# RMS norms of a two-layer encoder: the sum of squares of eight chunks taken from TensorE (eight ones-products) to GpSimd (seven f32 adds) and one ones-product

## The chip, the cores and the metric

The kernel runs on all eight cores of one Trainium2 chip, one batch element on each core, with no exchange between cores. The metric is device time in microseconds (us) of the slowest core, and a smaller number is better. Some runs fell into a second, slower state (about 1565 to 1795 us here, whatever the kernel): the cores of one die, or of both, show a lower granted clock in it. A "fast" run is one outside this state.

## The reference, cut to what matters

Five norms of this form stand in the network, over `x` of 2048 tokens by 1024 features per core:

```python
def rms_norm(x, g):
    xf = x.astype(jnp.float32)
    y = xf * lax.rsqrt(jnp.mean(xf * xf, axis=-1, keepdims=True) + EPS)
    return (y * g.astype(jnp.float32)).astype(x.dtype)

# layer 0:  x += attention(rms_norm(x))   norm 0    x += mlp(rms_norm(x))   norm 1
# layer 1:  x += conv(rms_norm(x))        norm 2    x += mlp(rms_norm(x))   norm 3
# output:   rms_norm(x)                   norm 4
def sq_relu_mlp(h, w_up, w_down):
    a = jax.nn.relu(h @ w_up)
    return (a * a) @ w_down
```

## The kernel before

Features lie on partitions: `x` is eight chunks of 128 partitions, in f32, and tokens are cut into four tiles of 512. A norm of one tile follows the tile's last matrix product. For each of eight chunks a matmul result is added to `x` on VectorE (`add_x`), the chunk is squared, and a product with a matrix of ones sums the squares over partitions. The eight ones-products accumulate in PSUM bank 7. Then ScalarE makes 1/rms of it (Ln, Exp), and eight `scalar_tensor_tensor` (STT below) on VectorE write `x * gain * rstd`.

```python
def norm_tile(gidx, src, c0, n, bank, out_fn, pool=False):
    for c in range(8):
        xa, xr = src(c)
        o, r_ = h_ap(c, c0, n), h_r(c, c0, n)
        alts = [("act", ... AF.Square ...), ("dve", ... i * i ...)]     # cut
        p.op(alts, None, [xr], [r_], None)
        MMS([(PS(bank, 0, n), onesN, o, c == 0, c == 7)], [CR1, r_], [PR(bank)])
    nb_ = nrs[ni[0] % 2]
    ni[0] += 1
    rs = nb_.ap[:, 0:n]
    ACT(rs, PS(bank, 0, n), AF.Ln, [PR(bank), sm.r()], [nb_.r(0, n)], n, bias=eps_ap)
    ACT(rs, rs, AF.Exp, [nb_.r(0, n)], [nb_.r(0, n)], n, scale=-0.5, ps=False)
    for c in range(8):
        out_fn(gidx, c, c0, n, src(c), nb_)

def norm_to_hT(gidx, c, c0, n, src, nb_):
    STT(h_ap(c, c0, n), src[0], gain_of(gidx, c),                       # shortened
        nb_.ap[:, 0:n], ALU.mult, ALU.mult, [...], [h_r(c, c0, n)], n)

def add_x(tt, c, lo, n, b):
    xa, xr = xs(tt, c, lo, n)
    TT("dve", xa, xa, PS(b, 0, n), ALU.add, [xr, PR(b)], [xr], n)

# the end of attention (norm 1); the ends of MLP 0 (norm 2), the convolution (norm 3)
# and MLP 1 (norm 4) have the same form
for tt in range(4):
    ...
    for oc in range(8):
        b = main.next()
        wo_mm(b, oc, tt, range(6), 0)
        wo_mm(b, oc, tt, (6, 7), 1)
        add_x(tt, oc, 0, 512, b)
    norm_x(1, tt, 0, 512, norm_to_hT)

# the start of an MLP
ACT(r.ap, PS(b), AF.Relu, [PR(b)], [r.r()], 512)
TT("pool", aT[i].ap[:, lo:lo + 512], r.ap, r.ap, ALU.mult, ...)
```

A list scheduler places the operations in the program, with an estimated cost for each, and so fixes one order of instructions per engine. An operation with alternatives gets its engine there too. At run time each engine follows its order and waits on semaphores. Matmul results go round seven PSUM banks.

## Time and profile before

| | before |
|---|---|
| time, median of 3 | 1534.3 us (1533.86 to 1534.9) |
| TensorE busy | 1471.2 us, 7312 matmuls |
| VectorE busy | 576.6 us |
| ScalarE busy | 490.7 us |
| GpSimd busy | 380.3 us |
| one 128x512 matmul | 0.2159 us |
| one STT of 128x512 | 0.74 us |

The first fence has three lines of the page of the kernel before: busy time, share and count of instructions of each engine; the chain of work that ended last, by engine; and the group of all STTs (L336 is the line of the STT helper): busy us, mean ns of one, then idle time of VectorE in front of them.

```profile
PE 1471.2 (96%) x7312; PEld 684.8 (45%) x7312; DVE 576.6 (38%) x820; ACT 490.7 (32%) x777; POOL 380.3 (25%) x387
...
PE 93%; DMA 2%; DVE 1%; ACT 1%; issue 1%; SPq 0%; POOL 0%; DVEq 0%; ACTq 0%; POOLq 0%
...
L336 DVE SCALAR_TENSOR_TENSOR arena<-arena 128x512 bf16<-128x512 f32 (+2 forms) x232 | 157.8, 738 | 24.8 <-ACT arena L328 19.7
```

TensorE is the bound, and GpSimd is idle for three quarters of the span. The chain in order of time (start, length, what) holds one piece that runs from the MLP of layer 0 through norm 2 and the convolution to the end of norm 3. L317 is the matmul helper:

```profile
412.63 663.21 PE psum L317 x3072
```

That is 663.21 / 3072 = 0.2159 us per matmul with nothing between them. A ones-product taken out of this piece shortens it by 0.2159 us, if nothing else changes.

The timeline of VectorE gives the four bursts of eight STTs that close the four tiles of norm 2:

```profile
798.55 5.38 DVE L336 SCALAR_TENSOR_TENSOR arena<-arena 128x512 bf16<-128x512 f32 x8
813.26 5.39 DVE L336 SCALAR_TENSOR_TENSOR arena<-arena 128x512 bf16<-128x512 f32 x8 [0.45 <-ACT arena L328]
829.63 5.38 DVE L336 SCALAR_TENSOR_TENSOR arena<-arena 128x512 bf16<-128x512 f32 x8
843.91 5.39 DVE L336 SCALAR_TENSOR_TENSOR arena<-arena 128x512 bf16<-128x512 f32 x8 [3.84 <-ACT arena L328]
```

Each takes 5.4 us. A tile gives VectorE eight adds of at most 0.69 us, this burst and at most one square: 11.6 us or less, in a tile of 72 matmuls, 15.5 us. VectorE has room.

The lines are of the convolution, from the timelines of both engines: a GpSimd product alone, then an STT and a GpSimd product that starts under it.

```profile
859.87 1.16 POOL L333 TENSOR_TENSOR arena<-arena 128x512 bf16<-128x512 bf16 x1 [4.02 <-DVE arena L336]
...
883.88 0.74 DVE L336 SCALAR_TENSOR_TENSOR arena<-arena 128x512 f32<-128x512 f32 x1
...
884.12 1.52 POOL L333 TENSOR_TENSOR arena<-arena 128x512 bf16<-128x512 bf16 x1 [0.18 <-DVE arena L336]
```

The GpSimd product takes 0.36 us longer; the STT still had 0.50 us to run when it began.

### The profile page before, as it was taken

How to read it: one execution, taken by the hardware profiler on the slowest of the kernel's cores; microseconds unless marked ns; L12 is line 12 of the kernel's file. 1: busy time of each engine (PE TensorE's matmuls, PEld its weight loads, DVE VectorE, ACT ScalarE, POOL GpSimd, SP SyncE). 2: the span in 40 equal slices, each digit the busy share in tenths (PEclk: the TensorE clock that was granted, in tenths of full speed). 3: DMA queues.
4: the chain of work that ended last, by engine and by line, in shares of the span. 5: the costliest groups of instructions: out<-in, count | busy, mean ns of one | idle time of the engine just before them, and what ended most of it. 6: DMA issues, size and time to landing. Idle time of an engine off the chain costs nothing.

```text
span 1531.6 us, 19902 instructions; the slowest of 8 cores (1524.7 to 1531.6 us)
## 1 busy us (share of the span) xinstructions
PE 1471.2 (96%) x7312; PEld 684.8 (45%) x7312; DVE 576.6 (38%) x820; ACT 490.7 (32%) x777; POOL 380.3 (25%) x387
## 2 busy tenths in 40 slices
PE   5999997699999999999999999999999999999997
PEld 2656443243344444444444444444444444444445
DVE  4646677556114013013036444456123023032047
ACT  3566686343320220310334333333310310301333
POOL 5100000100350540630620223210530621612600
PEclk8999999589999999999999999999999999999999
DMA  9944445630330420410410433310410411312014
GB/s 252 186 86 100 86 114 110 186 76 1 55 56 1 70 42 0 83 28 2 75 22 1 62 42 49 56 28 7 76 28 3 81 28 24 60 28 49 8 55 166
DMA packets 60910, 95.00 MB, mean 62 GB/s; under 512 B 3792, under 2 KB 40912, under 8 KB 58768
## 3 DMA queue, kind: packets, MB, share of 16 engines
q0 software_dynamic: 52016, 69.18, 25.9%
q1 hardware_dynamic: 8800, 24.55, 5.2%
q8 instruction: 61, 1.00, 0.3%
q14 instruction: 33, 0.27, 0.1%
HBM read 127.37 MB, written 8.52 MB: 89 GB/s over the span
## 4 chain that ended last, share of the span: by engine, by line
PE 93%; DMA 2%; DVE 1%; ACT 1%; issue 1%; SPq 0%; POOL 0%; DVEq 0%; ACTq 0%; POOLq 0%
PE psum L317 93%; DMA arena<-scr 2%; ACT arena L328 1%; DMA arena<-xT 1%; DVE arena L336 1%; DVE arena L333 1%; ACT arena L343 0%; SPq L349 0%; DMA scr<-arena 0%; POOL arena L349 0%; DVE arena L424 0%; DVE arena L345 0%; ACT arena L423 0%; DVEq L216 0%; ACTq L216 0%
## 5 line engine op out<-in xcount | busy, mean ns | idle before, releaser
L317 PE MATMUL psum<-arena 128*128 128x512 bf16 (+5 forms) x7312 | 1471.2, 366 | 52.7 <-DVE arena L333 16.6
L317 PEld LDWEIGHTS psum<-arena 128*128 128x128 bf16 (+1 forms) x7312 | 684.8, 101 | 838.9 <-issue 136.6
L333 DVE TENSOR_TENSOR arena<-arena,psum 128x512 f32<-128x512 f32 (+1 forms) x384 | 258.2, 684 | 819.6 <-PE psum L317 811.5
L328 ACT ACTIVATE arena<-psum 128x512 bf16<-128x512 f32 (+1 forms) x306 | 201.1, 668 | 649.0 <-PE psum L317 631.3
L333 POOL TENSOR_TENSOR arena<-arena 128x512 bf16<-128x512 bf16 x288 | 304.1, 1062 | 261.6 <-ACT arena L328 165.5
L336 DVE SCALAR_TENSOR_TENSOR arena<-arena 128x512 bf16<-128x512 f32 (+2 forms) x232 | 157.8, 738 | 24.8 <-ACT arena L328 19.7
L333 DVE TENSOR_TENSOR arena<-arena 128x2048 bf16<-128x2048 bf16 (+4 forms) x146 | 125.6, 905 | 37.8 <-ACT arena L328 25.7
L423 ACT ACTIVATE arena<-arena 128x512 bf16<-128x512 f32 (+1 forms) x143 | 83.7, 607 | 132.5 <-DVE arena L333 130.2
L349 POOL DMA_DIRECT2D arena<-wdn x16 | 12.4, 778 | 430.9 <-PE psum L317 430.9
L343 ACT CAST arena<-psum 128x512 bf16<-128x512 f32 (+2 forms) x149 | 87.1, 591 | 95.2 <-PE psum L317 89.9
L328 ACT ACTIVATE arena<-arena 128x512 f32<-128x512 f32 (+2 forms) x85 | 54.3, 657 | 68.6 <-DVE arena L333 54.3
L349 POOL DMA_DIRECT2D arena<-xT x18 | 13.4, 770 | 93.0 <-DVE arena L333 73.7
L343 ACT COPY arena<-psum 128x512 f32<-128x512 f32 x38 | 22.9, 601 | 41.0 <-PE psum L317 41.0
L345 DVE CAST arena<-psum 128x512 bf16<-128x512 f32 (+2 forms) x27 | 18.4, 683 | 42.5 <-PE psum L317 42.3
L328 ACT ACTIVATE arena<-psum,arena 128x512 f32<-128x512 f32 (+1 forms) x29 | 19.5, 673 | 35.5 <-PE psum L317 35.5
L349 POOL DMA_DIRECT2D arena<-wqk x8 | 7.4, 928 | 88.4 <-PE psum L317 88.4
L349 POOL DMA_DIRECT2D arena<-wup x16 | 15.0, 937 | 43.6 <-PE psum L317 38.9
L349 POOL DMA_DIRECT2D arena<-win x8 | 7.5, 932 | 71.8 <-PE psum L317 69.1
L511 ACT ACTIVATE arena<-arena 128x1024 bf16<-128x1024 bf16 x23 | 24.1, 1057 | 2.0 <-DVE arena L345 0.7
L349 POOL DMA_DIRECT2D arena<-wo x8 | 4.4, 549 | 52.1 <-PE psum L317 52.1
L424 DVE TENSOR_TENSOR arena<-arena 128x512 bf16<-128x512 f32 (+1 forms) x17 | 11.5, 684 | 14.0 <-DMA arena<-xT 13.0
L424 POOL TENSOR_TENSOR arena<-arena 128x512 bf16<-128x512 f32 x8 | 9.3, 1173 | 19.3 <-DMA arena<-xT 19.3
(14 smaller groups left out, 26.9 us busy)
## 6 DMA issues: line engine op xcount, KB each, us to landing
arena<-wup POOLq DMA_DIRECT2D x16, 1024.0 KB, 8.4
arena<-wdn POOLq DMA_DIRECT2D x16, 1024.0 KB, 12.0
arena<-xT POOLq DMA_DIRECT2D x14, 1024.0 KB, 9.8
arena<-arena SPq DMA_DIRECT2D x14, 512.0 KB, 5.1
arena<-scr SPq DMA_DIRECT2D x14, 512.0 KB, 7.2
arena<-win POOLq DMA_DIRECT2D x8, 768.0 KB, 7.3
outT<-arena SPq DMA_DIRECT2D x24, 256.0 KB, 2.5
arena<-wqk POOLq DMA_DIRECT2D x7, 512.0 KB, 10.9
```

The source lines that it names most:

```text
L317: i = e.matmul(o, lhsT=l, rhs=r, start=s0, stop=s1, skip_group_check=True)
L328: return p.op("act", lambda e: e.activation(out=out, in_=in_, func=func, **kw), R, W, c_act(n, ps) + (0.09 if scale is not None and not is ...
L333: return p.op(eng, lambda e: e.tensor_tensor(out=out, in0=in0, in1=in1, op=op), R, W, cost)
L336: return p.op("dve", lambda e: e.scalar_tensor_tensor(out=out, in0=in0, scalar=scalar, in1=in1, op0=op0, op1=op1), R, W, c_dve(n, False) + ...
L343: alts.append(("act", lambda e: e.copy(out=out, in_=in_), c_act(n) + more))
L345: alts.append((e_, lambda e: e.tensor_copy(out=out, in_=in_), c_dve(n, False) + more))
L349: return p.op(eng, lambda e: e.dma_start(out=out, in_=in_), R, W, 1.3 if eng == "sp" else 1.0, chan=chan, fill=fill, nbytes=nbytes)
L423: alts = [("act", lambda e, o=o, i=xa: e.activation(out=o, in_=i, func=AF.Square), c_act(n, False)), ("dve", lambda e, o=o, i=xa: e.tensor ...
L424: ("dve", lambda e, o=o, i=xa: e.tensor_tensor(out=o, in0=i, in1=i, op=ALU.mult), c_dve(n, False))]
L511: ("act", lambda e, o=sq.ap[:, sl], i_=rw.ap[:, sl]: e.activation(out=o, in_=i_, func=AF.Square), c_act(1024, False))], None, [rw.r(*rr)], ...
```

## The change

TensorE is the bound and GpSimd is idle around the norms. So the squares are now written in f32, GpSimd adds the eight of them up (seven adds; the last writes bf16), and TensorE multiplies the one sum by ones. It applies to tiles of 512 columns in norms 1 to 4: 15 tiles, of which each loses seven matmuls. The two tiles of 256 columns at the end of norm 4 keep the old form.

```diff
-        def norm_tile(gidx, src, c0, n, bank, out_fn, pool=False):
-
+        nsq = {lo: [B(U_V + lo + 1024 * i, 1024, True) for i in range(5)] for lo in (2048, 14336)}
+        nq = [0, 0]
+
+        def square_sum(gidx, src, c0, n, bank):
+
+            bufs = nsq[14336 if gidx == 4 else 2048]
+            acc = bufs[nq[0] % 2]
+            nq[0] += 1
             for c in range(8):
+                xa, xr = src(c)
+                t = acc
+                if c:
+                    t = bufs[2 + nq[1] % 3]
+                    nq[1] += 1
+                o, r_ = t.ap[:, 0:n], t.r(0, n)
+                p.op([("act", ... AF.Square ...), ("dve", ... i * i ...)], None, [xr], [r_], None)   # cut
+                if c:
+                    d, dr = (h_ap(0, c0, n), h_r(0, c0, n)) if c == 7 else (acc.ap[:, 0:n], acc.r(0, n))
+                    TT("pool", d, acc.ap[:, 0:n], o, ALU.add, [acc.r(0, n), r_], [dr], n)
+            MMS([(PS(bank, 0, n), onesN, h_ap(0, c0, n), True, True)], [CR1, h_r(0, c0, n)], [PR(bank)])
+
+        def norm_tile(gidx, src, c0, n, bank, out_fn, pool=False, on_pe=True):
+
+            if not on_pe:
+                square_sum(gidx, src, c0, n, bank)
+            for c in range(8 if on_pe else 0):
@@
-            norm_tile(gidx, lambda c: xs(tt, c, lo, n), tt * 512 + lo, n, 7, fn)
+            norm_tile(gidx, lambda c: xs(tt, c, lo, n), tt * 512 + lo, n, 7, fn, on_pe=n < 512)
```

More of the change, by code (lines that the diff above doesn't have):

```diff
@@ L416, in build_nc @@
         ni = [0]
-        def norm_tile(gidx, src, c0, n, bank, out_fn, pool=False):
-            for c in range(8):
+        nsq = {lo: [B(U_V + lo + 1024 * i, 1024, True) for i in range(5)] for lo in (2048, 14336)}
[4 more added lines that the diff above has]
+            nq[0] += 1
+            for c in range(8):
+                xa, xr = src(c)
[4 more added lines that the diff above has]
+                o, r_ = t.ap[:, 0:n], t.r(0, n)
+                p.op([("act", lambda e, o=o, i=xa: e.activation(out=o, in_=i, func=AF.Square), c_act(n, False)),
+                      ("dve", lambda e, o=o, i=xa: e.tensor_tensor(out=o, in0=i, in1=i, op=ALU.mult),
+                       c_dve(n, False))], None, [xr], [r_], None)
+                if c:
[6 more added lines that the diff above has]
+            for c in range(8 if on_pe else 0):
                 xa, xr = src(c)
```

## The prediction

> **What bounds the kernel now.** The chain that ended last is 93% TensorE. From 412.6 to 1075.9 us it is one unbroken piece, 3072 matmuls in 663.2 us: 0.2159 us per 128x512 matmul. That piece holds norm 2 and most of norm 3. GpSimd is 25% busy; the timeline shows it idle for over 50 us around each of norms 1 to 4.
>
> **What the change moves.** Norms 1, 2 and 3 have four 512-column tiles each, norm 4 three (its two 256-column halves keep the old form). Each of these 15 tiles loses seven ones-products: 105 matmuls x 0.2159 = 22.7 us, all where TensorE is the chain. The built program's order shows the same 105 gone. The squares stay on ScalarE (0.63 us) or VectorE (0.69 us), now with f32 output. GpSimd gains 7 f32 adds per tile. Norm 0's GpSimd squares of f32 took 1.173 us; I estimate 1.2 us per add, 8.4 us per tile. A tile of 65 matmuls takes 14.0 us, so GpSimd keeps up.
>
> **Contention.** The Trainium skill, "GPSIMD Engine Reference", section 8, says GpSimd shares its SBUF interfaces with VectorE and contends with VectorE instructions with two SBUF inputs. This trace agrees: a GpSimd product in the convolution takes 1.16 us alone and 1.53 us where about 0.5 us of it lies under a scalar_tensor_tensor (STT); an add from PSUM costs it nothing. The eight STTs that end each norm tile (5.4 us in a row) will nearly stop GpSimd, but VectorE then delivers no new chunk either, so GpSimd has about one add to do. I charge little.
>
> **What comes back.**
> 1. Each sum is ready later: the single ones-product stands 4 to 6 groups of eight matmuls (7 to 10 us) into the next tile's work in the new order. For norms 1 to 3 this is hidden: after the last tile's ones-product about 40 or more matmuls (over 8 us) precede the first that reads its result, which needs about 2 us (Ln 0.69, Exp 0.63, first STT 0.75). Squared-ReLU products queue behind the last adds, but three buffers and a spare bank cover that.
> 2. The tail is not hidden. Tile 2's eight final STTs began about 4 us after its projection ended, now about 10. VectorE, which ends the kernel, then has those 5.4 us, both halves' STTs (3.3 us each) and adds in one queue. Adding up, the end moves from 27.7 to 29.5 us after tile 2's projection: +2 us.
> 3. TensorE runs in an order fixed with estimated costs. Where GpSimd is later than assumed, TensorE stands at the ones-product: I allow 0 to 4 us over 15 tiles.
>
> **Prediction.** 1534.3 - 22.7 + 2 + 2 = 1515.6; say 1515.5 us, 1511 to 1523 to hold it 8 times in 10. Chances: faster by over 2% (below 1503.6) 0.02, which needs more than all of the removed work; within 2% 0.96; slower by over 2% 0.02.
>
> **What would show each step.** Matmuls 7312 to 7207; TensorE busy about 1449 us; GpSimd busy up by 120 to 140 us, its f32 adds near 1.2 us, longest under STT bursts; in the list of waits a new TensorE wait on GpSimd, below 4 us in total; windows over norms 2 and 3: 62 us become 56 us; the last STTs later after tile 2's projection.
>
> **What would make it wrong.** f32 adds above 1.7 us each, so that GpSimd falls behind the 1.73 us pace of a group and TensorE waits at each tile; STTs slowed by GpSimd, so that VectorE holds PSUM banks; a tail 5 us longer; or squared-ReLU products so late that ScalarE holds banks at the start of the MLP.

## More of the kernel before

The timeline of TensorE (start, busy length, what, count, and in brackets the idle time before and its releaser) shows the starts of the two MLPs, where TensorE waits for ScalarE to empty PSUM banks (L328 is the ScalarE helper):

```profile
396.60 7.07 PE L317 MATMUL psum<-arena 128*128 128x512 bf16 x32 [0.84 <-ACT arena L328]
...
1076.67 7.07 PE L317 MATMUL psum<-arena 128*128 128x512 bf16 x32 [0.84 <-ACT arena L328]
```

In norm 0 GpSimd squares some chunks in this kernel too. Here a square begins first, and an STT begins 0.05 us after it:

```profile
33.19 1.04 POOL L424 TENSOR_TENSOR arena<-arena 128x512 bf16<-128x512 f32 x1
...
33.24 1.54 DVE L336 SCALAR_TENSOR_TENSOR arena<-arena 128x512 bf16<-128x512 f32 x1 [2.56 <-ACT arena L328]
```

This STT takes 1.54 us instead of 0.74. Three of the eight STTs of that burst do so, and the burst takes 7.74 us instead of 5.4.

## The result

| | before | after |
|---|---|---|
| time, median of fast runs | 1534.08 us (4 runs) | 1524.85 us (4 runs, 1524.06 to 1525.36) |
| TensorE busy, matmuls | 1471.2 us, 7312 | 1454.9 us, 7207 |
| VectorE busy | 576.6 us | 602.4 us |
| GpSimd busy | 380.3 us | 520.4 us |

The ratio is 0.9939, with a 95% interval of 0.9921 to 0.9956. A ratio is the mean time of one kernel's fast runs over that of the other's of the same rounds, so it is not quite the ratio of the medians quoted. The gain is 9.2 us where 18.8 were predicted. The time lies above the range of the prediction (1511 to 1523).

The lines of the page after, as those of before:

```profile
PE 1454.9 (95%) x7207; PEld 674.7 (44%) x7207; DVE 602.4 (40%) x819; ACT 490.8 (32%) x778; POOL 520.4 (34%) x492
...
PE 89%; DVE 3%; DMA 3%; issue 2%; ACT 1%; POOL 1%; SPq 0%; DVEq 0%; ACTq 0%; POOLq 0%
...
L336 DVE SCALAR_TENSOR_TENSOR arena<-arena 128x512 bf16<-128x512 f32 (+2 forms) x232 | 181.6, 840 | 29.7 <-ACT arena L328 24.9
```

The 105 matmuls are gone. The chain has passed from TensorE in part to VectorE, 1% to 3%, and within it to the STTs. The same 232 STTs, of the same shapes, now take 181.6 instead of 157.8 us. The adds themselves, from the groups by shape:

```profile
L333 POOL TENSOR_TENSOR arena<-arena 128x512 f32<-128x512 f32 x90 | 118.7, 1320 | 99.6 <-ACT arena L433 90.8 <-POOL arena L333 5.9 <-DVE arena L434 1.5
```

**Where the gain was lost.** I cut the span of the slowest core at the same landmarks of VectorE in each trace: the first add to `x` in the attention's output projection, in MLP 0's first down projection, in its last one, in the convolution's output projection, in MLP 1's first down projection and in its last one, and the end. The third of the five intervals, inside MLP 0, holds no norm. "Expected" is 28 (norm 4: 21) matmuls times 0.2159 us.

| stage, us | before | after | gain | expected | lost |
|---|---|---|---|---|---|
| norm 1, to first down projection | 123.19 | 120.21 | 2.98 | 6.04 | 3.1 |
| norm 2, to the convolution's output | 229.64 | 226.46 | 3.18 | 6.04 | 2.9 |
| norm 3, to first down projection | 118.90 | 118.31 | 0.59 | 6.04 | 5.5 |
| norm 4, to the end | 70.86 | 71.36 | -0.50 | 4.53 | 5.0 |

So 22.65 us were taken out of TensorE's work and 16.4 came back in these two profiled runs, some in every norm. (By the medians of fast runs it is 22.65 - 9.2 = 13.4. The spans of the two profiled runs differ by 7.8 us; the four gains are 6.25 of them, and the other 1.55 lie before norm 1, where the landmark moves by up to 3.6 us from one run to another of any kernel. The last row ends at spans rounded to 0.1 us.)

**What a burst looks like now.** The four bursts of norm 2, as shown of before:

```profile
795.97 6.54 DVE L336 SCALAR_TENSOR_TENSOR arena<-arena 128x512 bf16<-128x512 f32 x8
813.72 7.41 DVE L336 SCALAR_TENSOR_TENSOR arena<-arena 128x512 bf16<-128x512 f32 x8
828.44 8.42 DVE L336 SCALAR_TENSOR_TENSOR arena<-arena 128x512 bf16<-128x512 f32 x8
843.32 5.39 DVE L336 SCALAR_TENSOR_TENSOR arena<-arena 128x512 bf16<-128x512 f32 x8 [3.22 <-ACT arena L328]
```

The first three, which run while the next tile's squares are added up, are 1.2, 2.0 and 3.0 us longer; the fourth, after which no tile follows, is not. The third one, instruction by instruction, beside GpSimd's adds of the same stretch (timelines of both engines, VectorE first):

```profile
828.44 1.76 DVE L336 SCALAR_TENSOR_TENSOR arena<-arena 128x512 bf16<-128x512 f32 x1
830.12 1.75 DVE L336 SCALAR_TENSOR_TENSOR arena<-arena 128x512 bf16<-128x512 f32 x1
831.80 1.75 DVE L336 SCALAR_TENSOR_TENSOR arena<-arena 128x512 bf16<-128x512 f32 x1
833.47 0.74 DVE L336 SCALAR_TENSOR_TENSOR arena<-arena 128x512 bf16<-128x512 f32 x1
```

```profile
828.38 1.27 POOL L333 TENSOR_TENSOR arena<-arena 128x512 f32<-128x512 f32 x1 [0.20 <-POOL arena L333]
829.86 1.47 POOL L333 TENSOR_TENSOR arena<-arena 128x512 f32<-128x512 f32 x1 [0.20 <-POOL arena L333]
831.53 1.47 POOL L333 TENSOR_TENSOR arena<-arena 128x512 f32<-128x512 f32 x1 [0.20 <-POOL arena L333]
```

The first STT begins 0.06 us after an add, and ends at 830.20, which is 0.55 us after the add has ended (829.65). The next add begins at 829.86, under that STT, and takes 1.47 instead of 1.27 us. The next STT begins at 830.12 under that add, and again ends about 0.55 us after it. The two engines take turns: whichever begins second gets done only after the first. In every such meeting of norms 1 to 4 in this trace a held STT ends 0.55 us after the add, and a held add 1.12 us after the STT. With no add left, an STT is back at 0.74 us. So an STT that meets an add loses about 1 us, and an add that meets an STT loses 0.2 to 0.45 us. The few squares on VectorE are held too (in norm 1 up to 1.60 us instead of 0.69).

This is what the Trainium skill states in "SBUF — State Buffer", section "SBUF: two separate sides": the port pair that VectorE and GpSimd share is "an **exclusive lock**, not a bandwidth split", held for the whole instruction by whoever starts first, for a VectorE instruction with two SBUF inputs against a GpSimd instruction that reads SBUF. This trace agrees: 0.74 us alone, 1.75 us held. The prediction used the one-line summary on another page, which names the contention and not who waits.

**How it reaches TensorE.** TensorE waits no longer for the STTs themselves (5.2 us in the list of waits, 6.0 before). The chain of after, from its last matmuls before norm 3's last tile closes to the start of MLP 1 (start, length, what):

```profile
1049.99 5.01 PE psum L317 x23
...
1055.90 7.13 DVE arena L336 x7
1063.02 0.61 DVE arena L333
...
1063.77 0.50 ACT arena L433
...
1064.90 0.59 ACT arena L328
1065.49 0.14 issue
1065.63 9.81 PE psum L317 x33
```

Tile 2's burst (8.81 us as a whole) holds back the adds to `x` of tile 3's last two chunks (L333; the chain shows the first). ScalarE's next instructions in its fixed order are the squares of these chunks (L433), and behind them stand the ReLUs (L328) that empty the banks of MLP 1's first matmuls. TensorE has run ahead into MLP 1, has filled its banks and waits. The starts of the two MLPs in TensorE's timeline, as shown of before:

```profile
390.17 8.97 PE L317 MATMUL psum<-arena 128*128 128x512 bf16 x33 [2.23 <-ACT arena L328]
...
1065.63 9.80 PE L317 MATMUL psum<-arena 128*128 128x512 bf16 x33 [3.73 <-ACT arena L328]
```

There is a second part to it. 33 matmuls at this place take 7.28 us at full clock (E3, below), and took 9.80. The windows around that start (columns: window, its length, busy us and count of five engines, granted TensorE clock, DMA share, GB/s), first of before, then of after:

```profile
core 7: us, PE busy (x) PEld busy (x) DVE busy (x) ACT busy (x) POOL busy (x), PEclk, DMA share, GB/s
1076.00:1080.00 4.00, 3.33 (x16) 1.59 (x17) 0.79 (x2) 2.10 (x4) 3.33 (x4) 1.00 1.12 211
```

```profile
core 7: us, PE busy (x) PEld busy (x) DVE busy (x) ACT busy (x) POOL busy (x), PEclk, DMA share, GB/s
1064.00:1068.00 4.00, 2.37 (x6) 0.87 (x7) 0.22 (x1) 2.46 (x5) 3.18 (x3) 0.50 1.02 141
1068.00:1072.00 4.00, 4.00 (x13) 1.50 (x12) 0.76 (x2) 1.92 (x3) 3.33 (x4) 0.66 1.13 216
```

The granted clock drops to 0.50 and 0.66 after the wait of 3.73 us. In before it is 1.00, after a wait of 0.84 us at the same place. So for norm 3: 3.73 - 0.84 = 2.9 us of longer wait, and 9.80 - 7.28 = 2.5 us of slower matmuls, together 5.4 of the 5.5 us lost. For norm 1: 2.23 - 0.84 = 1.4 and 8.97 - 7.28 = 1.7, together 3.1 of 3.1.

The wait is the same on all eight cores of this run, the fall of the clock is not. After the 2.23 us before MLP 0 it fell to 0.50 on five cores, for 3.41 us, and on three it did not fall; those three gain 4.5 us in norm 1 and not 3.0. After the 3.73 us before MLP 1 it fell on all eight, for 3.41 us on seven and for 6.83 us on the slowest, which the table shows; the seven gain 1.4 us in norm 3 and not 0.6.

In norm 2, TensorE stands still three times inside the norm:

```profile
825.62 10.74 PE L317 MATMUL psum<-arena 128*128 128x512 bf16 x49 [0.52 <-POOL arena L333]
837.61 3.40 PE L317 MATMUL psum<-arena 128*128 128x512 bf16 x15 [1.25 <-DVE arena L333]
841.33 39.01 PE L317 MATMUL psum<-arena 128*128 128x512 bf16 x180 [0.33 <-POOL arena L965]
```

That is 2.1 of the 2.9 us lost there; the rest I did not trace. Only the 0.52 us is a wait for an add of squares. The 1.25 us is a wait for VectorE's adds to `x`, which stood behind a burst.

How little room there is: a tile of 65 matmuls now takes 65 x 0.2159 = 14.03 us. VectorE's work for a tile was 11.6 us or less, and with a burst of 8.81 us it can be 15.0. But the trace does not show VectorE busy throughout: from the start of norm 3's second burst to that of its third it is busy 12.89 of 15.16 us. So it is not shown that VectorE as a whole became the bound. What the chain shows is a burst that stands in VectorE's order as one block, with two adds behind it that the start of the MLP waits for.

### The profile page after: what moved, and what is told of

It reads as the page before. It is cut to its first block, busy times and chain, and to the rows that moved or that the text cites. A ratio compares the mean times of both kernels' runs of the same rounds, so it can differ in the third digit from the quotient of the medians.

```text
span 1523.8 us, 20000 instructions; the slowest of 8 cores (1516.7 to 1523.8 us)
## 1 busy us (share of the span) xinstructions
PE 1454.9 (95%) x7207; PEld 674.7 (44%) x7207; DVE 602.4 (40%) x819; ACT 490.8 (32%) x778; POOL 520.4 (34%) x492
## 4 chain that ended last, share of the span: by engine, by line
PE 89%; DVE 3%; DMA 3%; issue 2%; ACT 1%; POOL 1%; SPq 0%; DVEq 0%; ACTq 0%; POOLq 0%
PE psum L317 89%; DVE arena L336 3%; DMA arena<-scr 2%; DMA arena<-xT 2%; ACT arena L328 1%; DVE arena L333 1%; POOL arena L333 0%; POOL arena L349 0%; ACT arena L343 0%; ACT arena L433 0%; SPq L349 0%; DMA scr<-arena 0%; POOL arena L449 0%; DVE arena L345 0%; DVEq L216 0%
## 5 line engine op out<-in xcount | busy, mean ns | idle before, releaser
L317 PE MATMUL psum<-arena 128*128 128x512 bf16 (+6 forms) x7207 | 1454.9, 366 | 61.1 <-ACT arena L448 18.3
L317 PEld LDWEIGHTS psum<-arena 128*128 128x128 bf16 (+2 forms) x7207 | 674.7, 101 | 841.0 <-issue 155.5
L333 DVE TENSOR_TENSOR arena<-arena,psum 128x512 f32<-128x512 f32 (+1 forms) x384 | 258.2, 684 | 782.6 <-PE psum L317 776.1
L333 POOL TENSOR_TENSOR arena<-arena 128x512 bf16<-128x512 bf16 (+2 forms) x393 | 443.0, 1133 | 340.0 <-ACT arena L328 151.7
L328 ACT ACTIVATE arena<-psum 128x512 bf16<-128x512 f32 (+1 forms) x306 | 201.4, 669 | 639.0 <-PE psum L317 618.6
L336 DVE SCALAR_TENSOR_TENSOR arena<-arena 128x512 bf16<-128x512 f32 (+2 forms) x232 | 181.6, 840 | 29.7 <-ACT arena L328 24.9
L333 DVE TENSOR_TENSOR arena<-arena 128x2048 bf16<-128x2048 bf16 (+4 forms) x146 | 127.9, 921 | 35.3 <-ACT arena L328 25.7
L433 ACT ACTIVATE arena<-arena 128x512 f32<-128x512 f32 x114 | 70.6, 631 | 153.4 <-DVE arena L333 136.2
L328 ACT ACTIVATE arena<-arena 128x512 f32<-128x512 f32 (+2 forms) x85 | 54.5, 659 | 65.3 <-DVE arena L333 51.0
L349 POOL DMA_DIRECT2D arena<-xT x18 | 13.4, 770 | 90.8 <-DVE arena L333 71.5
L328 ACT ACTIVATE arena<-psum,arena 128x512 f32<-128x512 f32 (+1 forms) x29 | 19.5, 672 | 15.2 <-PE psum L317 14.9
L448 ACT ACTIVATE arena<-arena 128x512 bf16<-128x512 f32 (+1 forms) x30 | 14.1, 523 | 9.2 <-DVE arena L333 7.0
```

Source lines behind the costliest of these rows:

```text
L317: i = e.matmul(o, lhsT=l, rhs=r, start=s0, stop=s1, skip_group_check=True)
L328: return p.op("act", lambda e: e.activation(out=out, in_=in_, func=func, **kw), R, W, c_act(n, ps) + (0.09 if scale is not None and not is ...
L333: return p.op(eng, lambda e: e.tensor_tensor(out=out, in0=in0, in1=in1, op=op), R, W, cost)
L336: return p.op("dve", lambda e: e.scalar_tensor_tensor(out=out, in0=in0, scalar=scalar, in1=in1, op0=op0, op1=op1), R, W, c_dve(n, False) + ...
L349: return p.op(eng, lambda e: e.dma_start(out=out, in_=in_), R, W, 1.3 if eng == "sp" else 1.0, chan=chan, fill=fill, nbytes=nbytes)
L433: p.op([("act", lambda e, o=o, i=xa: e.activation(out=o, in_=i, func=AF.Square), c_act(n, False)), ("dve", lambda e, o=o, i=xa: e.tensor_t ...
```

## The experiments

The theory (A): the adds hold up the STTs, VectorE falls behind, and this loses most of the 16.4 us (13.4 by the medians). Rivals: (B) the late sum, that is, the chain of seven adds, one ones-product, Ln and Exp is long, and everything behind it comes late whoever shares a port; (C) the order: the scheduler's costs for adds and STTs are wrong, so the fixed order is bad; (D) the loss is norm 4's, whose tail is not hidden. The times are medians of fast runs. The kernel before, beside these runs, was at 1534.27 (E1 to E4), 1533.30 (E5, E7 to E9) and 1532.70 us (E10, E11). All results were correct except E1's.

**E1: the squares stay as in the change, the adds are left out.** The sum is the last chunk's squares times eight (relative error 0.125).

```diff
+                if c == 7:
+                    o, r_ = h_ap(0, c0, n), h_r(0, c0, n)
                 p.op([("act", ...), ("dve", ...)], None, [xr], [r_], None)
-                if c:
-                    d, dr = ...
-                    TT("pool", d, acc.ap[:, 0:n], o, ALU.add, [acc.r(0, n), r_], [dr], n)
...
-            ACT(rs, PS(bank, 0, n), AF.Ln, ..., bias=eps_ap)
+            ACT(rs, PS(bank, 0, n), AF.Ln, ..., bias=eps_ap, scale=1.0 if on_pe else 8.0)
```

> The change without its GpSimd adds: squares as in the change, but only the eighth chunk's square (scaled by 8) goes into the one ones-product. Wrong result on purpose, magnitudes about right. If the GpSimd adds (their contention with VectorE's scalar_tensor_tensor (STT), and their chain) eat the gain, this shows what removing 105 ones-products is worth by itself: 1511 to 1514 us, STT of the norms back to 0.67 to 0.76 us, TensorE waits as before the change. If instead the removal itself leaves TensorE waiting (VectorE as the next limit, or a lower granted clock), the time stays at 1519 to 1525 us.

Measured: 1514.18 us (4 fast runs; ratio 0.9867, 0.9854 to 0.9881). The stages gain 6.02, 4.45, 6.05 and 3.31 us over before: norms 1 and 3 have all of their 6.04. So the adds cost about 10.7 us of time, and neither f32 squares nor the single ones-product does. It does not separate A from B, because the long chain went with the adds. (Norm 2's gain is 1.6 us short here. E3 has it in full.)

**E2: the kernel before, with 105 adds on GpSimd that nobody reads.** No matmul is removed, nothing waits for a sum.

```diff
...                                                                     # cut: acc, a buffer of its own
                 MMS([(PS(bank, 0, n), onesN, o, c == 0, c == 7)], [CR1, r_], [PR(bank)])
+                if gidx and n == 512 and c:
+                    pa, pr_ = src(0) if c == 1 else (acc.ap, acc.r())
+                    TT("pool", acc.ap, pa, xa, ALU.add, [pr_, xr], [acc.r()], n)
```

> The kernel before (all eight ones-products kept) plus the same 105 f32 GpSimd adds of 512 columns in norms 1 to 4, on x itself, whose sums nobody reads. If contention with VectorE is a main cost: VectorE's STT busy time rises by 10 to 25 us and the time by 2 to 8 us over before (1536 to 1542 us). If only the longer chain of the sum matters: the time stays within 1 us of before, since nothing waits for these sums. If GpSimd is the one that suffers, as predicted: STT unchanged, GpSimd adds above 1.5 us.

Measured: 1538.76 us (4 fast runs; ratio 1.0029, 1.0016 to 1.0043), +4.5 us; stages 0, 1.5, 0 and 2.1 us longer. The STTs that write bf16, from the groups by shape:

```profile
L336 DVE SCALAR_TENSOR_TENSOR arena<-arena 128x512 bf16<-128x512 f32 x128 | 111.3, 937 | 16.6 <-ACT arena L328 16.4
```

They are at 937 ns on average, where before had 763 and after 921 by the same view. So adds that nobody waits for hold up the STTs in full, and it costs 4.5 us, though nothing in norms 1 and 3. E2 is no exact copy of the change's collisions: its third bursts of norms 1 to 3 take 5.38, 7.21 and 6.38 us (change: 8.02, 8.42, 8.81), and its longest stand fourth. The third bursts also stand earlier: norm 3's begins 19.3 us before TensorE's start into MLP 1, in the change 11.4 us before. The removal of matmuls without adds loses nothing in norms 1 and 3 (E1), and neither does the hold without removal and without the late sum (E2). Whether a held burst is dear in the change because the tile is shorter or because the late sum puts the burst closer to the MLP, no run separates.

**E3: the change, with 1/rms left in PSUM for norms 1 to 3.** Ln and Exp work in place in bank 7, and the STT reads it there. The STT then has one input in SBUF instead of two. The chain, the adds and their number stay the same. A token guards bank 7 until the last STT has read it, so the chain is, if anything, longer. The order of instructions of TensorE, and in the traces of VectorE, ScalarE and GpSimd too, is the change's, row for row.

```diff
...                                                                     # cut: the ones-product also writes the token
+            if not on_pe and gidx < 4:
+                rs, tok = PS(bank, 0, n), (2, 310000, 310064)
+                ACT(rs, rs, AF.Ln, [PR(bank), sm.r()], [PR(bank)], n, bias=eps_ap)
+                ACT(rs, rs, AF.Exp, [PR(bank)], [PR(bank), tok], n, scale=-0.5)
+                for c in range(8):
+                    xa, xr = src(c)
+                    STT(h_ap(c, c0, n), xa, ..., rs, ALU.mult, ALU.mult, [xr, sm.r(), tok], [h_r(c, c0, n)], n)
+                return
```

> The change, but in norms 1 to 3 Ln and Exp leave the reciprocal root in PSUM bank 7 and the STTs read it there, so each STT has one SBUF tensor input instead of two. The GpSimd adds, their chain and the single ones-product stay. Contention theory: the STTs of norms 1 to 3 fall back to about 0.67 to 0.7 us whatever GpSimd does, the TensorE waits before the MLPs vanish, and 5 to 10 us come back: 1515 to 1520 us. Chain theory (the sum simply comes too late): STTs may be faster, but the time stays above 1522 us.

Measured: 1515.81 us (4 fast runs; ratio 0.9879, 0.9866 to 0.9893). Stages: gains of 6.05, 6.03 and 6.04 us, all of the expected 6.04 each, and -0.49 in norm 4, which this edit does not touch. A burst of norm 2 and two adds that run beside it, from the timelines:

```profile
826.69 5.35 DVE L336 SCALAR_TENSOR_TENSOR arena<-arena,psum 128x512 bf16<-128x512 f32 x8
```

```profile
826.71 1.27 POOL L333 TENSOR_TENSOR arena<-arena 128x512 f32<-128x512 f32 x1 [0.20 <-POOL arena L333]
828.19 1.26 POOL L333 TENSOR_TENSOR arena<-arena 128x512 f32<-128x512 f32 x1 [0.20 <-POOL arena L333]
```

The adds and the burst overlap, and neither takes longer for it. The start of MLP 1 in TensorE's timeline is as before, with 33 matmuls in 7.28 us:

```profile
1059.05 7.28 PE L317 MATMUL psum<-arena 128*128 128x512 bf16 x33 [0.84 <-ACT arena L328]
```

This settles norms 1 to 3 for A and against B as a cause by itself: with the same late sum and without the hold, nothing is lost. As the order is also the same, it speaks against C. (The adds are freed by it as well, but their mean goes only from 1320 to 1284 ns.) It agrees with the Trainium skill, "SBUF — State Buffer", section "Who interferes with whom", which says that a VectorE instruction with at most one SBUF input, outside the two-port modes, does not contend with GpSimd.

**E11: the control for E3.** The kernel before (all ones-products) with 1/rms in PSUM for norms 1 to 3.

> Control for e3_rstd_psum: the kernel before (eight ones-products, no GpSimd adds), with Ln and Exp of norms 1 to 3 left in PSUM bank 7 and read there by the STTs. If the gain of e3_rstd_psum over the change comes from keeping STTs clear of GpSimd, this brings nothing here: 1533 to 1537 us (a little slower is possible, since the next tile's ones-products must wait for bank 7). If PSUM operands were a gain of their own: 1526 to 1530 us.

Measured: 1532.78 us (3 fast runs; ratio 0.9999, 0.9981 to 1.0017). An operand in PSUM by itself is worth nothing here. E3's gain is the end of the hold.

**E4: norm 4 in the old form, norms 1 to 3 changed.**

```diff
-            norm_tile(..., 7, fn, on_pe=n < 512)
+            norm_tile(..., 7, fn, on_pe=gidx == 4)
```

> The change in norms 1 to 3 only; norm 4 keeps eight ones-products per tile. It loses 21 x 0.216 = 4.5 us of removed matmuls. From the traces the stretch from the start of the last down projection to the end took 70.9 us before and 71.4 us after, so if norm 4's change is a wash as that says, the time is within 1.5 us of the change (1523 to 1526 us), and the last stretch again 70.9 us. If norm 4 gained its predicted 2.5 us, the time is 1527 us.

Measured: 1525.69 us (5 fast runs; ratio 0.9944, 0.9930 to 0.9957), less than 1 us from the change; the intervals overlap. So D falls: norm 4's part is worth about zero and is not what costs 9 us. Norm 4 loses as much as its removed matmuls had given.

**E5: the last tile of each norm in the old form, and all of norm 4.** The third burst is then met by no adds.

```diff
+            norm_tile(..., 7, fn, on_pe=gidx == 4 or tt == 3)
```

> The change in tiles 0 to 2 of norms 1 to 3 only: the last tile of each and all of norm 4 keep eight ones-products and put no adds on GpSimd. 63 matmuls are removed (13.6 us). If the loss comes from adds of tile t+1 standing in the way of tile t's STTs, the burst of tile 2, which is followed by no adds now, is back at 5.4 us, the TensorE waits and the low granted clock before the two MLPs vanish, and norms 1 and 3 gain their full 4.5 us each: 1521 to 1523 us. If the loss lies in all tiles alike, the gain shrinks in proportion: 1526 to 1528 us.

Measured: 1522.81 us (4 fast runs; ratio 0.9928, 0.9908 to 0.9947). Norms 1 to 3 gain 4.11, 3.63 and 3.74 of 4.53 us (21 matmuls each), and TensorE's wait before MLP 0 and MLP 1 is 1.27 us with the clock at full speed (32 matmuls in 7.07 us). With fewer matmuls removed it is faster than the change in these stages. This fits a loss in norms 1 and 3 that lies mostly in the held third burst, the last one that adds of a following tile meet. By itself E5 would not tell this from the last tile's late sum, which is gone too; E3, which has that sum and no loss, does.

**E9: the change with dearer costs for the scheduler alone.** Adds are planned at `n + 53` columns, and the STTs at 0.35 us more. The work is the same in another order; but the scheduler also moved four squares from ScalarE to VectorE (VectorE 823 instructions, change 819).

```diff
-                    TT("pool", d, ..., [dr], n)
+                    TT("pool", d, ..., [dr], n + 53)
...
+                if not on_pe:
+                    s_.cost += 0.35
```

> The change, with the list scheduler told what the trace shows: an add 0.1 us dearer, an STT of norms 1 to 4 behind GpSimd adds 0.35 us dearer. The arithmetic and the count of instructions are the change's; only the order differs. If the loss is an order built on wrong costs, most of it comes back: below 1519 us. If VectorE simply cannot run its STTs while GpSimd adds (exclusion), the order can't give that back: 1522 to 1527 us.

Measured: 1533.49 us (4 fast runs; ratio 1.0003, 0.9985 to 1.0020). I expected at most 1527, and missed. The scheduler moved the ones-product later, so that two bursts stood nearly back to back in VectorE's timeline:

```profile
1047.91 7.40 DVE L336 SCALAR_TENSOR_TENSOR arena<-arena 128x512 bf16<-128x512 f32 x8
1056.74 5.39 DVE L336 SCALAR_TENSOR_TENSOR arena<-arena 128x512 bf16<-128x512 f32 x8 [1.43 <-ACT arena L328]
1062.05 4.95 DVE L333 TENSOR_TENSOR arena<-arena,psum 128x512 f32<-128x512 f32 x8
```

From 1047.3 to 1062.05 us no add to `x` is done, the banks stay full, and TensorE waits 4.08 us for VectorE before MLP 1 (and 3.95 before MLP 0). So the order, with those four squares, can lose as much as the whole change gains. Dearer costs are no cure: with them this scheduler makes the order worse, not better. What speaks against C is E3, which has the change's order and no loss. Whether a better order for the held STTs exists stays open.

**E10: the squares and the partial sums in bf16.** The same adds with fewer bytes.

```diff
-        nsq = {lo: [B(U_V + lo + 1024 * i, 1024, True) ...
+        nsq = {lo: [B(U_V + lo + 1024 * i, 512) ...
```

> The change with squares and running sums kept in bf16 instead of f32: every GpSimd add reads and writes half the bytes. If VectorE's STT is held for the length of an overlapping add, it is held a little less, since bf16 products on GpSimd took 1.04 us against 1.27 us for the f32 adds: held STTs near 1.5 us instead of 1.75, and 1 to 4 us come back (1521 to 1524 us). If only f32 traffic collides: STTs stay at 0.74 us and the time falls to 1515 to 1518 us.

Measured: 1517.39 us (3 fast runs; ratio 0.9900, 0.9878 to 0.9921), where I expected 1521 to 1524, and missed. An add takes 1.16 us (f32: 1.27), and an STT that meets one 1.64 us (f32: 1.75). So the hold is not one of bytes or of f32. It is shorter by as much as the add is. Yet 6 us (by the ratios to before) to 8 us (by the spans of the profiled runs, 1515.4 against 1523.8) came back for 0.11 us per add. Norms 1 and 2 lose 0 and 0.5 us. Norm 3 loses 3.2 on the slowest core, which is one of three whose clock fell, and 1.5 on the other five. The third burst of norm 3, and TensorE's start into MLP 1:

```profile
1048.45 8.36 DVE L336 SCALAR_TENSOR_TENSOR arena<-arena 128x512 bf16<-128x512 f32 x8
...
1059.41 8.97 PE L317 MATMUL psum<-arena 128*128 128x512 bf16 x33 [2.34 <-ACT arena L328]
```

Each engine's order is the change's here as in E3, so the three runs can be set side by side. Shorter adds end sooner, and fewer of them meet a burst: one instead of two STTs are held in norm 1's third burst, two instead of three in norm 2's. The third bursts and TensorE's waits before the MLPs are 5.34 us and 0.84 us in E3 (both norms); 6.85 and 0.84 in norm 1 here; 8.02 and 2.23 in norm 1 of the change; 8.36 and 2.34 in norm 3 here; 8.81 and 3.73 in norm 3 of the change. So the wait begins to grow somewhere between a burst of 6.85 and one of 8.02 us, and a hold shorter than that costs nothing there. That a small change of the adds gives back so much fits this; no run tests it by itself.

**E7: as E3, and also norm 4's tiles 0 and 1 with 1/rms in PSUM.**

```diff
+            if not on_pe and (gidx < 4 or c0 < 1024):
+                nb_ = _PsumRs(PS(bank, 0, n))        # then Ln, Exp in place, STT from PSUM
```

> As e3_rstd_psum, and also for tiles 0 and 1 of norm 4; tile 2 of norm 4 keeps its root in SBUF, since bank 7 is wanted by the half tiles then. Contention theory: the two bursts of norm 4 (6.54 and 7.42 us in e3_rstd_psum) fall to 5.4 us, the TensorE wait of 1 us there goes, and the tail starts earlier: 2 to 3.5 us below e3_rstd_psum, 1513 to 1514.5 us. If the tail is set by the late sum of tile 2 alone: within 1 us of e3_rstd_psum.

Measured: 1512.86 us (3 fast runs; ratio 0.9867, 0.9848 to 0.9887). Norms 1 to 3 are as in E3, and the tail is 69.82 us (E3: 71.35). So 1.5 of the 5.0 us that norm 4 lost were the hold on the bursts of its tiles 0 and 1.

**E8: as E7, but norm 4's third tile in the old form.**

```diff
-            norm_tile(..., 7, fn, on_pe=n < 512)
+            norm_tile(..., 7, fn, on_pe=gidx == 4 and tt >= 2)
```

> As e7_psum_all_but_last, but tile 2 of norm 4 keeps its eight ones-products, so no GpSimd add stands behind the last full tile. It has 7 matmuls more (1.5 us), but tile 2's STTs can start earlier. If the late sum of tile 2 costs the tail more than 1.5 us: faster than e7_psum_all_but_last, 1512 to 1513.5 us; if not, 1 to 1.5 us slower.

Measured: 1512.58 us (4 fast runs, 1511.48 to 1512.99; ratio 0.9864, 0.9847 to 0.9882). It beats before by about 21 us and the change by about 12. From E7 it differs by 0.3 us, with overlapping intervals: these runs don't tell the two apart.

**What is left of norm 4.** Its stage lost 5.0 us. By differences of profiled runs: 1.5 us are the hold on tiles 0 and 1 (E3 against E7). 2.3 us lie between E7 (69.82) and E1 without any adds (67.55). There tile 2's own sum is late. Its STTs are not held: in the change they run as one string with seven of the first half's, 8.15 us for 15, where unheld ones of before would be 5.39 + 7/8 x 3.25 = 8.2. In before that burst starts at 1508.08 and the half's STTs follow at 1518.70, after a gap. E8, which undoes this one tile, has a stage of 69.15, 0.7 us shorter than E7 although it does 1.5 us of matmuls more. Both fit a cost of about 2.3 us for the late sum, the rival B, in this one place; but E8's order differs too, so this is argued. The last 1.2 us are lost even in E1 and stay open.

## Why the prediction was wrong

- **The removed work was right.** 105 matmuls of 0.2159 us, all on the chain: norms 1 to 3 gain exactly 6.04 us each as soon as nothing is given back (E3).
- **GpSimd's load was right, its adds a little dear.** The prediction had 1.2 us per add and 120 to 140 us in all; it was 1.27 us plus 0.20 us between dependent adds, and 140 us.
- **The step that failed is "Contention".** In its words: the STTs "will nearly stop GpSimd, but VectorE then delivers no new chunk either, so GpSimd has about one add to do. I charge little." GpSimd stops VectorE too, and by more: an STT under an add went from 0.74 to 1.75 us, an add under an STT from 1.27 to 1.47. The conv evidence, 1.16 to 1.53 us, showed only the case in which the STT had begun first, and I took the one direction for the rule; norm 0 of the same trace had the other (1.54 us). Also it was not one add: one, two and three adds met the first three bursts of norm 2, because a chain of seven dependent adds trails behind the chunks. No time was charged for held STTs, and they came to +23.8 us.
- **The terms of the sum.** "0 to 4 us", taken as 2, for TensorE waiting at the ones-products, against 3.1 + 2.9 + 5.5 = 11.5 us measured in norms 1 to 3 for the waits of another kind. "+2 us" for the tail measured 5.0 us: about 2.3 for the late sum that it was meant for, if the differences above are read so, 1.5 for the hold, and 1.2 open. Against 22.65 us removed, 16.4 us came back in the profiled runs (13.4 by the medians) where 4 had been charged.
- **The wait was looked for in the wrong place.** The prediction named "a new TensorE wait on GpSimd, below 4 us". In the list of waits it is 0.5 us. The loss stands as a wait on ScalarE's ReLU, whose total went from 6.2 to 10.5 us, because the delay passes from GpSimd to VectorE, to ScalarE's queue, to the banks. The prediction's last paragraph named the right mechanism, "STTs slowed by GpSimd, so that VectorE holds PSUM banks", as a thing that would make it wrong, and gave it no room in the range.
- **Not foreseen at all: the clock.** 2.5 us in norm 3 and 1.7 us in norm 1, on the slowest core, are matmuls at a lower granted clock after a wait. A wait of 2.23 us can cost more than its length here, as it did on five of eight cores; one of 3.73 us did on all.
- **What was right about the chain.** The late sum is hidden in norms 1 to 3, as item 1 of "What comes back" said (E3 loses nothing with it).

## What to carry to other kernels

Before work goes to GpSimd because it is idle, look at what VectorE does at the same moments: an instruction there with two SBUF inputs waits out a whole GpSimd instruction, about 1 us each time here. An operand moved to PSUM ends it (E3: 9 us). And work off TensorE shortens the time that every other engine has per tile, so ask what stands behind the slowed burst in its engine's order, and who waits for that. Look in the trace for both orders of two colliding instructions: the convolution showed one here, and norm 0 the other.

## What the Trainium skill lacked or had wrong

- "GPSIMD Engine Reference", section 8: the key point names contention with VectorE instructions that have two SBUF inputs, but not who waits, nor does it point to "SBUF — State Buffer", which has the rule. The runs show a wait either way: an STT takes 1.75 us under an add and not 0.74, an add 1.47 to 1.72 us under an STT and not 1.27.
- "SBUF — State Buffer", section "Who interferes with whom": right, but with no cost per meeting. Here a chain of dependent adds, with 0.20 us between two, and a burst of STTs take turns one for one: +1.2, +2.0 and +3.0 us for one, two and three adds. An STT ends 0.55 us after the add that held it. With bf16 adds, which are 0.11 us shorter, a held STT is so too (1.64 us). It also does not name an operand in PSUM as a remedy for STTs, which brought the bursts back to 5.35 us.
- "TensorE: Matmul & The Clock Gate", section "HAM oscillation — how this bites in real kernels": it gives as the rule "no PE-idle gaps >~3.4µs". Here a shorter gap could be enough: the granted clock fell to 0.50 after the gap of 2.23 us before MLP 0 on five of eight cores, and after one of 2.34 us (E10) on three of eight, with 33 matmuls in 8.97 us instead of 7.28. After gaps of 0.84 to 1.27 us before the MLPs it fell on none. Norm 3's gap of 3.73 us, with a fall on all eight cores, agrees with the rule.
